# Lending finished mixer buffers to the rows of u and v in a two-layer diffusion backbone

## The chip, the core and the metric

The kernel runs on one core of one Trainium2 chip. The metric is the time of one execution on the device in microseconds (us). The core's engines are TensorE (PE; its weight loads are listed as PEld), VectorE (DVE), ScalarE (ACT), GpSimd (POOL) and SyncE (SP). Transfers go through 16 DMA engines; those of this text are issued by SP (weights) and by POOL (gathers of rows).

## What is computed

Two layers run over 256 latent tokens and 256 context tokens of width 1024, in float32. Each layer has a token mixer (window attention, differential attention, a convolution and a pooling branch, each with a gate) and then a feed-forward part that looks up experts. The change concerns the second part, `peer_ffn`:

```python
q = (xc @ wq).reshape(PEER_CHUNK, PEER_HEADS, 2, PEER_DKEY // 2)
...
gate = jax.nn.softmax(sc.astype(jnp.float32), axis=-1).astype(xc.dtype)
u = jnp.take(u_tab, idx, axis=0)
act = jax.nn.gelu(jnp.einsum('td,thkd->thk', xc, u), approximate=False)
v = jnp.take(v_tab, idx, axis=0)
return jnp.einsum('thk,thkd->td', gate * act, v)
```

Each token has 8 heads, each head picks 16 of 16384 experts. So each token needs 128 rows of u and 128 rows of v, 4 KB each.

## The kernel before, in words

The tokens are four tiles of 128: tiles 0 and 1 are context, 2 and 3 latents. Layer 1 runs the expert part for all four, layer 2 only for the latents, so there are six passes of it. A pass is the generator `gather` (L1114): for h = 0 to 8 it hands out 16 slots each. Slot k of step h fetches row h*16+k of u (`u_slot`, L1001, up to h = 7) and row (h-1)*16+k of v (`v_slot`, L1016, from h = 1): the v rows run one head behind, since their weights need the whole head. The first 16 slots are thus u alone and the last 16 v alone.

One gather (L998) is one instruction of POOL: it takes 128 indices and fetches one 4 KB row for each partition into a tile of 128 x 1024. A u row is multiplied by the token's vector and summed by one DVE instruction (L1006). After 16 of them `weigh` (L1009) forms the weights on ACT and DVE. A v row is either added to a sum by DVE (L1023) or multiplied with a diagonal matrix by PE (four matmuls of L1030, the matrix made by ACT, L1028). Which of both is fixed for each pass: in the latents' first pass of a layer (`few`) every fourth row goes to DVE, in the second (`half`) every second one. `add` (L1041) puts the sums into the tokens at the pass's end.

The rows lie in tiles of the tag "u" or "v" with GB = 5 places each. A gather may start when the row that was in its place has been read: by DVE for u, by DVE or PE for v.

The indices come from `route` (L1053), one head at a time: products with the query weights and the keys on PE, then `select` (L919), a search for the 16 best on DVE. In the latents' passes the routes of the following heads run beside the first pass (`side`), one at each step h. In layer 1 their weights come through the tag "w". In layer 2 those of heads 0 to 5 are fetched earlier and kept (`keep_q`, L1381) in tiles that the mixer no longer needs: head 0 in kc0 and vc0, head 1 in kc1 and vc1, head 2 in a tile hT, head 3 in two tiles q, head 4 in ys2 and ys3, head 5 in hk and ys0. ys1 is read by the mixer's last product, `mix(1, 1)`.

A pass that stands in the list `behind` is handed out in small portions while other work is emitted: `pump(us)` adds us times `credit[1]`, and each SLOT_US = 2.9 hands out a slot. `drain()` hands out the rest at once. The layer-1 latents start with a drain of the context's pass (L1313), then come both their passes (L1315, L1316). In layer 2 the first pass is put into `behind` at L1410 with RATE2 = 0.753; then `mix(1, 1)` (8 products, 1.8 each), `out_proj` (8 products, 2 each) and one `norm_T` (4) are emitted, the routes of heads 2, 0 and 1 (the last two for tile 3 alone), and the drain (L1419); the second pass is L1420.

The framework puts the instructions of each engine into an order when the program is built. It goes by the order of emission and by when it reckons data and places to be there, so an instruction that waits can be passed by later ones. On the chip each engine then keeps to that order.

Of the kernel before, what the change touches and what calls it, by code (L numbers as in the profile page):

```python
# [8 lines left out]
F = mybir.dt.float32  # L9
# [8 lines left out]
D = 1024  # L18
# [19 lines left out]
GB = 5  # L38
# [10 lines left out]
def body(ctx: ExitStack, tc: tile.TileContext, x_d, cc_d, cols_d, rows_d, w_mod, w_in, w_gate,  # L49
# [5 lines left out]
    sb = ctx.enter_context(tc.tile_pool(name="sb", bufs=1))  # L55
    pp = ctx.enter_context(tc.tile_pool(name="ps", bufs=1, space=bass.MemoryType.PSUM))

    def mm_ps():
        return pp.tile([128, 512], F, tag="mm", name="mm", bufs=2)
# [4 lines left out]
    def tr_ps():  # L64
        return pp.tile([128, 512], F, tag="tr", name="tr", bufs=2)
# [4 lines left out]
    def t2():  # L70
        return sb.tile([128, 512], F, tag="t2", name="t2", bufs=4)

    def m4(w=T):
        return sb.tile([128, 4, w], F, tag="m4", name="m4", bufs=3)
# [79 lines left out]
    def drain():  # L154
        while behind:
            for _ in behind.pop(0):
                pass
# [66 lines left out]
    def wtile(src, kb=KB, c=256, like=None):  # L224

        src = src.rearrange("(k p) c -> p k c", p=128)
        w = wplace(kb, c)
        nc.sync.dma_start(w, src)
        if not isinstance(like, Split):
            return w  # L230
        return Split(parts_of(w), row_places(kb // 2), row_places(kb // 2))
# [85 lines left out]
    def hslot():  # L317
        return sb.tile([128, KB, T], F, tag="hT", name="hT", bufs=3)
# [403 lines left out]
    def ch_proj(hT, l, c0, w=None):  # L722

        N = hT.shape[2]
        w = w or wtile(w_in[l, :, c0:c0 + 256], like=hT)
        ps = mm_ps()
        for b in range(2):
            product(ps[:, b * N:(b + 1) * N], w, slice(b * 128, (b + 1) * 128), hT, slice(0, N))
        tick(TICKS[0])
        pump(N * 7 / T)  # L730
        return ps[:, :2 * N].rearrange("p (b t) -> p b t", b=2)
# [68 lines left out]
    def pool_in(hT, l, ws=(None,) * 2):  # L800
        PAD = 16
        W = T + 2 * PAD
        u = m4(W)
        nc.vector.memset(u[:, :, :PAD], 0.0)  # L804
        nc.vector.memset(u[:, :, PAD + T:], 0.0)
        for i in range(2):
            pd = ch_proj(hT, l, O_DI + i * 256, ws[i])
            nc.scalar.copy(u[:, 2 * i:2 * i + 2, PAD:PAD + T], pd)
        return u

    def pool(u, l, out_):

        PAD = 16
        W = T + 2 * PAD
        pw = t2().rearrange("p (g c) -> p g c", g=4)
        nc.sync.dma_start(pw, pool_w[l].rearrange("g c e -> c g e"))

        a = m4(W)
        src = u
        for g, win in enumerate(WINS):  # L820
            w = W - win + 1
            h = win // 2
            nc.vector.tensor_tensor(a[:, g:, :w], src[:, g:, :w], src[:, g:, h:h + w], op=OP.add)
            lo = PAD - h
            y = t2()[:, :T]
            nc.vector.tensor_tensor(y[:, :8], a[:, g, lo:lo + 8], rcp[:, g, :8], op=OP.mult)
            nc.scalar.mul(y[:, 8:T - 8], a[:, g, lo + 8:lo + T - 8], 1.0 / win)
            nc.vector.tensor_tensor(y[:, T - 8:], a[:, g, lo + T - 8:lo + T], rcp[:, g, 8:], op=OP.mult)
            nc.vector.tensor_tensor(y, y, u[:, g, PAD:PAD + T], op=OP.subtract)
            ps = tr_ps()  # L830
            nc.tensor.matmul(ps[:, :T], pw[:, g, :], y, start=True, stop=True)
            nc.scalar.activation(out_[:, g, :], ps[:, :T], AF.Copy, scale=cols[:, l, C_PS + g:C_PS + g + 1])
            src = a
            yield
# [129 lines left out]
    def second_layer():  # L964

        nc.vector.tensor_scalar(places16[:, 0], places16[:, 0], float(NEXP // 128), None, op0=OP.add)

    class Tile:


# [23 lines left out]
            self.dacc = sb.tile([128, D], F, tag="dacc", name="dacc", bufs=1)  # L994

        def row(self, table, tag, j):
            r = sb.tile([128, D], F, tag=tag, name=tag, bufs=GB)
            nc.gpsimd.indirect_dma_start(out=r, out_offset=None, in_=table,  # L998
                                         in_offset=bass.IndirectOffsetOnAxis(ap=self.idx[:, j:j + 1], axis=0))
            return r  # L1000
# [52 lines left out]
    def route(ts, l, h, hT, c0, later=None, w=None):  # L1053

        w = w or wtile(w_q[l, :, h * 256:(h + 1) * 256])
        kt = sb.tile([128, 256], F, tag="kt", name="kt", bufs=1)
        nc.sync.dma_start(kt, kt_d[l, :, h])
        N = len(ts) * 128
        qT = []
        for b in range(2):  # L1060
            ps = mm_ps()
            product(ps[:, :N], w, slice(b * 128, (b + 1) * 128), hT, slice(c0, c0 + N))
            q = sb.tile([128, T], F, tag="qT", name="qT", bufs=2)
            nc.scalar.copy(q[:, :N], ps[:, :N])
            qT.append(q)
        jobs, scs = [], []
        for i, t in enumerate(ts):
            sp = mm_ps()
            for b in range(2):
                nc.tensor.matmul(sp[:, b * 128:(b + 1) * 128], qT[b][:, i * 128:(i + 1) * 128],  # L1070
                                 kt[:, b * 128:(b + 1) * 128], start=True, stop=True)
            sc = sb.tile([128, 256], F, tag="sc", name="sc", bufs=2)
            nc.scalar.copy(sc, sp[:, :256])
            if later is not None and t.t == 1:
                nc.scalar.dma_start(later[h], sc)
                continue
            jobs.append((t, h))
            scs.append(sc)
        if jobs:
            select(jobs, scs)  # L1080
# [20 lines left out]
    def waited(t, later):  # L1101

        for h in range(0, 8, 2):
            scs = [sb.tile([128, 256], F, tag="sc", name="sc", bufs=2) for i in range(2)]
            for i, sc in enumerate(scs):
                nc.scalar.dma_start(sc, later[h + i])
            select([(t, h), (t, h + 1)], scs)
            yield 1
            yield 1

    def gather(t, on_dve, nxt=None, side=()):

        side = iter(side)
        t.begin(on_dve)  # L1114
        for h in range(9):
            next(side, None)
            if h == 8:
                t.gates()
            for k in range(16):
                if h < 8:  # L1120
                    t.u_slot(h * 16 + k)
                if h > 0:
                    t.v_slot(h * 16 - 16 + k)
                yield 1
            if h < 8:
                t.weigh(h)
            if h == 7 and nxt:
                nxt.prepare()
        for _ in side:
            pass  # L1130
        t.add(t.va.rearrange("p a b -> p (a b)"))

    def ysb(n):
        return sb.tile([128, 4, T], F, tag=f"ys{n}", name=f"ys{n}", bufs=1)
# [43 lines left out]
    def part(y, n):  # L1178
        return y[:, :, n * 128:(n + 1) * 128]
# [16 lines left out]
    def pieces(gen, n):  # L1196

        pending.extend([lambda: next(gen, None)] * n)
# [3 lines left out]
    ys = [ysb(n) for n in range(4)]  # L1202
    alloc_kv((1,))
    u = pool_in(hc, 0)
# [12 lines left out]
    def every(*gens):  # L1217
        for g in gens:
            for _ in g:
                pass  # L1220
# [36 lines left out]
    def place(tag, bufs=1):  # L1257
        return sb.tile([128, D], F, tag=tag, name="wk", bufs=bufs).rearrange("p (k c) -> p k c", k=4)

    places = [[place("dacc"), place("h2", 2)]] + [[place("v", GB) for i in range(2)] for j in range(2)]  # L1260
# [4 lines left out]
    h = hslot()  # L1265
# [12 lines left out]
    u = pool_in(h, 0, ws[4:6])  # L1278
    alloc_kv((0,))
    ys = [ysb(n) for n in range(4)]  # L1280
# [29 lines left out]
    tsl = []  # L1310
    rl = router((2, 3), 0, tsl)
    next(rl)
    drain()  # L1313

    every(gather(tsl[0], P_L0, tsl[1], rl))  # L1315
    every(gather(tsl[1], P_L1, tsc[1], waited(tsc[1], later)))  # L1316


    behind.append(gather(tsc[1], P_C1))
    credit[1] = RATE1  # L1320
    h = norm_T((2, 3), 1, 0)
    hx = norm_T((0,), 1, 0, hk())
    alloc_kv((0, 1))
    yb = conv_in(h, 1)
    u = pool_in(h, 1)
    pieces(pool(u, 1, ys[3]), 5)
    pieces(conv(yb, 1, ys[2]), 16)
    kv_proj(h, 1, hx)
# [27 lines left out]
    def cut(n):  # L1356
        return slice(n * 128, (n + 1) * 128)

    def mix(n, br):
        th = (tha, thc)[br]  # L1360
        branches(part(ys[br], n), 128, lambda blk: th[blk // 4][:, blk % 4, cut(n)], accT[:, :, cut(n)], wbr[br])
# [37 lines left out]
    route(tsl[:1], 1, 0, hT, 0, w=wq[0])  # L1399
    tsl[0].prepare(True)  # L1400

    def routes():

        yield 1
        yield 1
        for h in range(3, 8):
            route(tsl, 1, h, hT, 0, w=wq[h] if h < len(wq) else None)
            yield 1

    behind.append(gather(tsl[0], P_F0, tsl[1], routes()))  # L1410
    credit[1] = RATE2
    mix(1, 1)
    route(tsl[:1], 1, 1, hT, 0, w=wq[1])
    out_proj(accT[:, :, cut(1)], (3,), 1, wout)
    norm_T((3,), 1, 1, hT, 128)
    route(tsl, 1, 2, hT, 0, w=wq[2])
    for h in range(2):
        route(tsl[1:], 1, h, hT, 128, w=wq[h])
    drain()  # L1419
    every(gather(tsl[1], P_F1))  # L1420

# [2 lines left out]
    for n in range(2):  # L1424
        r = st8()[:, 7:8]
# [68 lines left out]
```

## Time and profile before

| what | value |
|---|---|
| median of 3 runs | 3164.84 us (3161.33 to 3167.96) |
| the profiled execution | 3163.87 us |
| its span, first to last instruction | 3162.1 us |
| DVE busy | 2332.2 us (74%) |
| PE busy | 2358.6 us (75%) |
| POOL busy | 1760.0 us (56%) |
| gathers of u, busy on POOL | 768, 869.1 us, mean 1132 ns |
| gathers of v, busy on POOL | 768, 890.3 us, mean 1159 ns |
| DMA bytes | 1036.55 MB, of which gathers 805.40 MB |

Shares of the span are averages over stages with different limits. The latents' passes are at 1016 to 1784 us (layer 1) and 2391 to 3145 us (layer 2). The trace lists for each idle time of an engine what ended it; "issue" is time in which it waited for nothing that the trace shows. Between two gathers POOL always has such a step of about 0.3 us.

### The profile page before, as it was taken

How to read it: one execution, taken by the hardware profiler on the slowest of the kernel's cores; microseconds unless marked ns; L12 is line 12 of the kernel's file. 1: busy time of each engine (PE TensorE's matmuls, PEld its weight loads, DVE VectorE, ACT ScalarE, POOL GpSimd, SP SyncE). 2: the span in 40 equal slices, each digit the busy share in tenths (PEclk: the TensorE clock that was granted, in tenths of full speed). 3: DMA queues.
4: the chain of work that ended last, by engine and by line, in shares of the span. 5: the costliest groups of instructions: out<-in, count | busy, mean ns of one | idle time of the engine just before them, and what ended most of it. 6: DMA issues, size and time to landing. Idle time of an engine off the chain costs nothing.

```text
span 3162.1 us, 33260 instructions
## 1 busy us (share of the span) xinstructions
PE 2358.6 (75%) x10524; PEld 1568.2 (50%) x10524; DVE 2332.2 (74%) x5221; ACT 667.9 (21%) x1577; POOL 1760.0 (56%) x1542
## 2 busy tenths in 40 slices
PE   7999998889867776675555479679997876545555
PEld 5878887667755552222111267557686542211111
DVE  5956569778977899856677659876657995556776
ACT  3455421224112121110000111023332221110001
POOL 0000037544555577777777657666405687767775
PEclk9999999999988897786788799889998987977868
DMA  9948969887899899998999999999957899989998
GB/s 307 318 142 263 315 229 322 300 306 263 316 359 335 310 391 326 334 375 323 396 409 407 332 336 384 322 346 354 344 167 264 290 325 366 397 315 397 407 408 312
DMA packets 436782, 1036.55 MB, mean 328 GB/s; under 512 B 30464, under 2 KB 226560, under 8 KB 436608
## 3 DMA queue, kind: packets, MB, share of 16 engines
q0 software_dynamic: 221184, 805.40, 67.9%
q1 hardware_dynamic: 211984, 226.25, 21.5%
q10 hardware_dynamic: 3440, 2.78, 0.3%
q8 instruction: 84, 1.38, 0.2%
q14 instruction: 90, 0.74, 0.1%
HBM read 1032.22 MB, written 2.10 MB: 327 GB/s over the span
## 4 chain that ended last, share of the span: by engine, by line
PE 29%; issue 23%; DVE 22%; DMA 18%; POOL 7%; ACT 1%; ACTq 0%; POOLq 0%; DVEq 0%
PE mm L215 12%; DVE u L1006 6%; DMA v<-in_v_dram,idx 6%; DMA u<-in_u_dram,idx 4%; DMA w<-in_w_gate_dram 4%; POOL u L998 3%; POOL v L998 3%; PE va L1030 3%; DVE m L774 3%; DVE dacc L1023 3%; DMA w<-in_w_in_dram 2%; PE mm L213 2%; PE mm L211 2%; PE mm L212 2%; PE at L473 2%
## 5 line engine op out<-in xcount | busy, mean ns | idle before, releaser
L998 POOL DMA_INDIRECT u<-in_u_dram,idx x768 | 869.1, 1132 | 919.0 <-DVE m L804 430.9
L1030 PE MATMUL va<-v,dg 128*128 128x512 f32 x1436 | 871.0, 745 | 568.7 <-DMA v<-in_v_dram,idx 493.0
L1006 DVE SCALAR_TENSOR_TENSOR u<-u,h 128x1024 f32<-128x1024 f32 x768 | 934.7, 1220 | 328.3 <-DMA u<-in_u_dram,idx 326.2
L998 POOL DMA_INDIRECT v<-in_v_dram,idx x768 | 890.3, 1159 | 465.0 <-issue 172.7
L1030 PEld LDWEIGHTS va<-v,dg 128*128 128x128 f32 x1436 | 304.7, 230 | 1071.4 <-issue 853.4
L1023 DVE SCALAR_TENSOR_TENSOR dacc<-v,wt,dacc 128x1024 f32<-128x1024 f32 x403 | 515.9, 1280 | 105.5 <-DMA v<-in_v_dram,idx 91.0
L215 PE MATMUL mm<-hT,w 128*128 128x256 f32 (+1 forms) x2176 | 512.4, 387 | 108.1 <-DMA w<-in_w_gate_dram 70.5
L215 PEld LDWEIGHTS mm<-hT,w 128*128 128x128 f32 x2176 | 407.9, 204 | 184.7 <-issue 69.6
L1028 ACT ACTIVATE dg<-ident,wt 128x128 f32<-128x128 f32 x359 | 141.5, 400 | 965.8 <-PE va L1030 906.0
L774 DVE SCALAR_TENSOR_TENSOR m<-m,cols,m 128x256 f32<-128x256 f32 x360 | 158.0, 475 | 0.1
L212 PE MATMUL mm<-hT,whi 128*128 128x256 f32 x512 | 143.9, 281 | 0.8 <-DVE hT L174 0.8
L211 PE MATMUL mm<-hT,whi 128*128 128x256 f32 x448 | 128.1, 286 | 4.0 <-ACT whi L173 3.2
L213 PE MATMUL mm<-hT,whi 128*128 128x256 f32 x448 | 127.2, 284 | 1.2 <-DVE whi L174 0.8
L215 PE MATMUL mm<-w,hT 128*128 128x256 f32 x512 | 116.3, 386 | 9.4 <-DMA w<-in_w_in_dram 9.4
L174 DVE TENSOR_TENSOR whi<-w,whi 128x1024 fp32r<-128x1024 f32 x86 | 104.1, 1222 | 17.6 <-ACT whi L173 10.3
L215 PEld LDWEIGHTS mm<-w,hT 128*128 128x128 f32 x512 | 98.5, 194 | 25.0 <-issue 11.2
L173 ACT CAST whi<-w 128x1024 fp32r<-128x1024 f32 x86 | 88.4, 1048 | 68.0 <-PE mm L213 46.3
L215 PE MATMUL mm<-ys,w 128*128 128x256 f32 x384 | 95.0, 385 | 4.6 <-ACT th L844 4.0
L212 PEld LDWEIGHTS mm<-hT,whi 128*128 128x128 f32 x512 | 97.4, 190 | 1.7 <-DVE hT L174 1.0
L844 ACT ACTIVATE th<-mm,cols 128x256 f32<-128x256 f32 x80 | 37.9, 474 | 261.6 <-PE mm L215 204.8
L211 PEld LDWEIGHTS mm<-hT,whi 128*128 128x128 f32 x448 | 85.6, 191 | 6.4 <-ACT whi L173 4.0
L213 PEld LDWEIGHTS mm<-hT,whi 128*128 128x128 f32 x448 | 85.1, 190 | 6.8 <-DVE whi L174 3.6
(339 smaller groups left out, 2821.3 us busy)
## 6 DMA issues: line engine op xcount, KB each, us to landing
w<-in_w_gate_dram SPq DMA_DIRECT2D x48, 1024.0 KB, 10.7
w<-in_w_in_dram SPq DMA_DIRECT2D x42, 1024.0 KB, 10.6
X<-in_w_mod_dram SPq DMA_DIRECT2D x40, 512.0 KB, 5.2
wm<-in_w_mod_dram SPq DMA_DIRECT2D x40, 512.0 KB, 5.3
w<-in_w_branch_dram SPq DMA_DIRECT2D x20, 1024.0 KB, 8.0
w<-in_w_q_dram SPq DMA_DIRECT2D x20, 1024.0 KB, 12.0
u<-in_u_dram,idx POOLq DMA_INDIRECT x768, 6.5
v<-in_v_dram,idx POOLq DMA_INDIRECT x768, 6.5
```

What stands on the lines that cost most here:

```text
L173: nc.scalar.copy(hi.bitcast(FR), v)
L174: nc.vector.tensor_tensor(lo.bitcast(FR), v, hi, op=OP.subtract)
L211: nc.tensor.matmul(ps, ah, bh, start=first, stop=False)
L212: nc.tensor.matmul(ps, ah, bl, start=False, stop=False)
L213: nc.tensor.matmul(ps, al, bh, start=False, stop=last)
L215: nc.tensor.matmul(ps, a[:, kb, ca], b[:, kb, cb], start=first, stop=last)
L774: nc.vector.scalar_tensor_tensor(acc[:, b, :], yb[:, b, k:k + T], cols[:, l, cw + k:cw + k + 1], acc[:, b, :], op0=OP.mult, op1=OP.add)
L998: nc.gpsimd.indirect_dma_start(out=r, out_offset=None, in_=table, in_offset=bass.IndirectOffsetOnAxis(ap=self.idx[:, j:j + 1], axis=0))
L1006: nc.vector.scalar_tensor_tensor(r, r, 1.0, self.h2, op0=OP.mult, op1=OP.mult, accum_out=self.act[:, j % 16:j % 16 + 1])
L1023: nc.vector.scalar_tensor_tensor(self.dacc, v, w, self.dacc, op0=OP.mult, op1=OP.add)
L1028: nc.scalar.activation(dg, ident, AF.Copy, scale=w)
L1030: nc.tensor.matmul(self.va[:, half, :], dg, v[:, half * 512:(half + 1) * 512], start=j == self.pe[0], stop=j == self.pe[-1])
```

## The change

A list of tags for each table, `places_of`, says where the next rows go, in turn. `row` takes its tile from `row_place`. For layer 1's latents u gets seven more places (ys0 to ys3, two of q, hk) and v four (kc0, vc0, kc1, vc1), lent before the drain; `give_back` returns to five and five after the second pass. Layer 2 then allocates its ys tiles anew, where before it wrote into those of layer 1. In layer 2 places are lent one after the other: ys1 after `mix(1, 1)`, and those of kept query weights each time the last route that reads them has been emitted. At the end u has 14 and v 7.

```diff
+    places_of = {"u": ["u"] * GB, "v": ["v"] * GB}
+    turn = {"u": 0, "v": 0}
+
+    def lend(**more):
+
+        for tag, places in more.items():
+            places_of[tag].extend(places)
+
+    def give_back():
+        for tag in "uv":
+            places_of[tag] = [tag] * GB
+            turn[tag] = 0
+
+    def row_place(tag):
+        at = places_of[tag]
+        place = at[turn[tag] % len(at)]
+        turn[tag] += 1
+        return sb.tile([128, D], F, tag=place, name=tag, bufs=GB if place in "uv" else 2 if place == "q" else 1)
...
         def row(self, table, tag, j):
-            r = sb.tile([128, D], F, tag=tag, name=tag, bufs=GB)
+            r = row_place(tag)
...
     next(rl)
+    lend(u=["ys0", "ys1", "ys2", "ys3", "q", "q", "hk"], v=["kc0", "vc0", "kc1", "vc1"])
     drain()
 
     every(gather(tsl[0], P_L0, tsl[1], rl))
     every(gather(tsl[1], P_L1, tsc[1], waited(tsc[1], later)))
+    give_back()
...
     u = pool_in(h, 1)
+    ys = [ysb(n) for n in range(4)]
     pieces(pool(u, 1, ys[3]), 5)
...
+    freed = {0: dict(u=["kc0"], v=["vc0"]), 1: dict(u=["kc1", "vc1"]), 3: dict(u=["q", "q"]),
+             4: dict(u=["ys2"], v=["ys3"]), 5: dict(u=["hk", "ys0"])}
+
     def routes():
 
         yield 1
         yield 1
         for h in range(3, 8):
             route(tsl, 1, h, hT, 0, w=wq[h] if h < len(wq) else None)
+            lend(**freed.get(h, {}))
             yield 1
 
     behind.append(gather(tsl[0], P_F0, tsl[1], routes()))
     credit[1] = RATE2
     mix(1, 1)
+    lend(u=["ys1"])
     route(tsl[:1], 1, 1, hT, 0, w=wq[1])
...
     for h in range(2):
         route(tsl[1:], 1, h, hT, 128, w=wq[h])
+        lend(**freed[h])
     drain()
     every(gather(tsl[1], P_F1))
```

## Rows read from the trace of the kernel before

**Rows 1.** Stretches: PE, PEld, DVE, ACT, POOL busy us, TensorE clock, DMA share, GB/s.
```profile
1100.00:1240.00 140.00, 104.23 (x316) 57.45 (x316) 138.52 (x464) 26.57 (x63) 100.86 (x86) 0.88 0.99 369
1240.00:1300.00 60.00, 36.93 (x56) 12.72 (x54) 59.79 (x212) 8.14 (x18) 49.03 (x37) 0.74 0.91 317
1300.00:1404.00 104.00, 71.00 (x112) 25.77 (x112) 61.74 (x98) 13.37 (x33) 81.45 (x74) 0.79 0.98 365
1404.00:1447.00 43.00, 31.85 (x77) 14.13 (x76) 18.99 (x27) 7.42 (x19) 23.61 (x26) 0.89 0.90 328
...
1500.00:1750.00 250.00, 132.63 (x193) 43.97 (x192) 177.46 (x247) 20.56 (x54) 191.21 (x193) 0.81 1.02 404
...
2465.00:2600.00 135.00, 111.37 (x377) 66.58 (x376) 130.60 (x445) 28.03 (x68) 104.62 (x82) 0.93 0.90 319
```

**Rows 2.** Waits of POOL, 1016 to 1105 us: total us, times, longest.
```profile
POOL u L998 <- DVE u L1006: 10.2, 8, 3.5
...
POOL v L998 <- PE va L1030: 6.2, 2, 5.4
```

**Rows 3.** Waits of POOL, 1105 to 1240 us.
```profile
POOL v L998 <- PE va L1030: 8.2, 8, 2.2
POOL u L998 <- DVE u L1006: 6.2, 7, 1.7
```

**Rows 4.** Waits of POOL, 1240 to 1404 us.
```profile
POOL v L998 <- PE va L1030: 1.8, 6, 0.3
...
POOL u L998 <- DVE u L1006: 0.6, 1, 0.6
```

**Rows 5.** POOL's timeline: tile ends' u rows, and the last v row.
```profile
1404.53 1.01 POOL L998 DMA_INDIRECT u<-in_u_dram,idx  x1 [0.31 <-issue]
...
1436.44 0.94 POOL L998 DMA_INDIRECT u<-in_u_dram,idx  x1 [0.30 <-issue]
...
1755.14 0.94 POOL L998 DMA_INDIRECT u<-in_u_dram,idx  x1 [0.30 <-issue]
...
1783.27 0.94 POOL L998 DMA_INDIRECT u<-in_u_dram,idx  x1 [0.31 <-issue]
...
2764.32 1.02 POOL L998 DMA_INDIRECT u<-in_u_dram,idx  x1 [0.30 <-issue]
...
2796.96 0.94 POOL L998 DMA_INDIRECT u<-in_u_dram,idx  x1 [0.30 <-issue]
...
3115.32 0.94 POOL L998 DMA_INDIRECT u<-in_u_dram,idx  x1 [0.30 <-issue]
...
3143.65 0.94 POOL L998 DMA_INDIRECT v<-in_v_dram,idx  x1 [0.64 <-DVE dacc L1023]
```

**Rows 6.** Waits of POOL, 2510 to 2764 us, longest in total.
```profile
POOL v L998 <- PE va L1030: 3.0, 10, 0.3
```

**Rows 7.** Timeline of DVE and POOL near 1331 us, of PE at 1358.
```profile
1331.40 1.23 DVE L1006 SCALAR_TENSOR_TENSOR u<-u,h 128x1024 f32<-128x1024 f32 x1 [1.98 <-DMA u<-in_u_dram,idx]
1331.88 1.56 POOL L998 DMA_INDIRECT v<-in_v_dram,idx  x1 [0.30 <-issue]
...
1358.03 1.96 PE L1030 MATMUL va<-v,dg 128*128 128x512 f32 x4 [0.21 <-DMA v<-in_v_dram,idx]
```

**Rows 8.** DMA issues: count and median us from issue to landing.
```profile
v<-in_v_dram,idx POOLq DMA_INDIRECT x768, 6.5
```

**Rows 9.** Waits of POOL, 1404 to 1447 us.
```profile
POOL u L998 <- DVE u L1006: 3.3, 2, 2.6
```

**Rows 10.** Timeline of POOL and PE at the beginning of layer 2's latents.
```profile
2405.49 0.94 POOL L998 DMA_INDIRECT u<-in_u_dram,idx  x1 [1.73 <-DVE u L1006]
2434.78 2.07 PE L1030 MATMUL va<-v,dg 128*128 128x512 f32 x2 [17.27 <-ACT dg L1028]
2457.58 4.03 PE L215 MATMUL mm<-hT,wk 128*128 128x128 f32 x32
2462.97 1.83 POOL L998 DMA_INDIRECT v<-in_v_dram,idx  x1 [10.05 <-PE mm L1070]
```

## The prediction

> **What bounds the kernel now.** I read the stretches first. In the expert stages GpSimd (POOL) issues 256 gathers of 128 rows per tile (128 of u, 128 of v). Where nothing holds it, 193 gathers take 250 us, 1.295 us each, at 404 GB/s and a DMA share of 1.02 [rows 1]: the fastest pace the kernel knows. I call it the free pace; there the gathers themselves are the limit and no number of places helps.
>
> The two latent tiles of layer 1 hold POOL from about 1016 to 1784 us: 768 us for 512 gathers that would take 663 at the free pace. So some 105 us are not pace; in layer 2 it is 2391 to 3145, 754 us, so some 91. Then I asked where POOL loses them and what it waits for, since only a wait for a *place* can shrink.
> - 1016 to 1240 us: POOL waits for VectorE (DVE) to finish a u row (10.2 and 6.2 us) and for TensorE to finish a v row (6.2 and 8.2) [rows 2, 3]: 31 us, all waits for one of the five places per table. DVE is itself busy 138.5 of 140 us [rows 1].
> - 1240 to 1404 us: place waits are gone (0.6 us for u) [rows 4], yet a gather takes 1.62 us up to 1300 (60 us, 37) and 1.41 after (104 us, 74) [rows 1].
> - At the end of each tile: the last u row is issued, 17 v rows follow alone, then 16 u rows of the next tile alone. Five places per table hold POOL then. From the last u row to the next pass's first are 18 gathers: 31.9 us in layer 1, 32.6 in layer 2, and 28.1 at the end of layer 1's second tile; to the kernel's last v row are 17, 28.3 us [rows 5]. At the free pace 18 gathers take 23.3 us and 17 take 22.0.
> - Layer 2's first tile, 2510 to 2764: POOL waited for nothing longer than 0.3 us (the longest row sums ten such steps) [rows 6]. Only its first 70 us and its end can change.
>
> **The sum.** The added code issues no instruction on the chip: Python picks another tag, and DVE, TensorE, ScalarE and the transfers have the same work. What moves is the moment at which POOL may issue. The sum is against the profiled execution, 3163.87 us (span 3162.1); the median of the runs is 1 us above, so I add 1.
> 1. *First tile of layer 1.* u has 12 places, v 9. DVE sets the pace until 1300, so that end stays; what changes is how far POOL stands ahead then. u and v are issued in turn, so the shorter list counts: 9 pairs ahead for 5, 8 gathers. After 1300 POOL is behind DVE (61.7 of 104 us busy), so each gather already issued is worth its 1.41 us: 8 x 1.41 = 11. There is idle time to issue them in: 31 us of place waits [rows 2, 3]. Ends: 0, if the lead is used up before 1300, and 20, if all seven added u places count (14 gathers). I take 6, as gathers are dearer while DVE has a backlog (below).
> 2. *Layer 1, tile to tile.* The v rows become bound by TensorE: 12 of 16 go there (every fourth to DVE) at 1.96 us [rows 7], 24 us, rather than by five places and a landing of 6.5 us [rows 8]. 31.9 - 24 = 8. POOL's wait behind the first u rows (3.3 us, [rows 9]) goes as well, since 12 places hold them while DVE adds the tile up: 2.5. Together 10.5; ends 4 and 13.
> 3. *Layer 1, end of the second tile.* 28.1 - 23.3 = 5: half the rows go to each engine, 8 x 1.96 = 16 us, so TensorE doesn't bind. Ends 1 and 5. What follows is the mixer of layer 2, which needs the tile's sum: the stage is shifted whole.
> 4. *Background tile, layer 2's mixer:* 5 and 5 places again, nothing. The new ys tiles wait for u rows read long before: nothing; the cover is the 16 v rows behind them.
> 5. *Layer 2, beginning.* Here is the doubtful step. Counting the credit: 8 branch products x 1.8, 8 output products x 2 and one norm x 4 are 34.4, times 0.753 over 2.9 gives 8 slots handed out before the drain. Row 8 of u therefore gets place 8 of nine: vc1, which holds query weights of head 1 until tile 3's product of that head. That product starts at 2457.58 and takes 4.03 us, to 2461.6; the present kernel issued u rows at 2405.49 and fed the first v row to TensorE at 2434.78 [rows 10]. Head 0's v rows need all 16 u rows, so they come some 35 us later. The build lets other rows pass (rows 9 to 14 have free places), and POOL now stands still for 10 of those us anyway [rows 10]. I take 0 between -10 and +8.
> 6. *Layer 2, tile to tile.* 32.6 - 24 = 8.6, and 2.4 at the first u rows, as in 2: 11. Seven v places still carry it: 6.5 us landing and 2 of use over 7 rows are 1.2 us a row. Ends 4 and 14.
> 7. *End of the kernel.* 28.3 - 22 = 6; ends 2 and 6.
>
> Sum: 6 + 10.5 + 5 + 0 + 11 + 6 = 38.5, say 39 us: 3163.9 - 39 + 1 = **3126 us**. Who is late next: POOL, at its free pace, and at the tile ends TensorE.
>
> **Why gathers are dearer beside a busy DVE.** A gather usually takes 0.94 us. The one of 1331.88 took 1.56: a product of a u row had begun on DVE at 1331.40 and ended at 1332.63, and the gather ends 0.81 us after it [rows 7]. So a gather that starts inside a product waits it out. The Trainium skill's page "SBUF — State Buffer" (section "SBUF: two separate sides") says that DVE, in an instruction with two SBUF inputs, and GpSimd take one port pair as an exclusive lock, whoever starts first. The trace agrees, by that pair of instructions. By that rule a change that lets rows pile up in front of DVE makes DVE's products run back to back and so slows POOL; that is the second rival below.
>
> **Rivals.**
> - *The lent places stall POOL in layer 2 (slower).* Each engine runs in the order written at build time; if that order puts row 8 or a row in q, ys or hk before its weights are really read, POOL stands still with everything behind it. Price: held from 2405.5 to 2462.5, 57 us, of which it waits 10 today, so 47; and some 19 u products of 1.23 us [rows 7], 23 us, then fall into 2465 to 2600, where DVE is busy 130.6 of 135 us [rows 1]. 70 - 39 = 31 slower: 3196. It decides once the stall costs more than the 39 us of the other steps. For it: the 10 us wait on a route product [rows 10] shows that the built order can be wrong. Against: only one row in three of the first lists is lent before 2462. 0.14, of which 0.10 slower by over 0.2%.
> - *The port takes it back.* Rows land earlier, DVE runs dense, a gather costs 1.62 us as in 1240 to 1300 [rows 1]. 18 gathers then take 29.2, 17 take 27.5: the four tile ends give 2.7 + 0 + 3.4 + 0.8 = 7 us, step 1 nothing: 3158. For it: just that stretch. Against: in the tile ends DVE has few rows to do (19.0 of 43 us busy) [rows 1]. 0.14.
> - *More than forecast.* Steps 1, 2, 3, 5, 6, 7 at their upper ends: 20 + 13 + 5 + 8 + 14 + 6 = 66: 3099; by halves between that and the forecast, 3110. 0.12.
> - *It does nothing it says*: that rows never reach the lent places is excluded by the code, which cycles through the list from the drain on.
>
> **The numbers.** Forecast 0.60. About 0.2% (6 us) is what a measurement of this kernel tells from no change. Faster: 0.60 + 0.12 + 0.07 of the port case = 0.79; same: 0.07 of the port case and 0.04 of the stall = 0.11; slower 0.10. The range goes from 3099, the larger gain, to 3160, past the port case; the stall and what lies beyond all upper ends are left out, some 0.15.
>
> **What would show it.** Right: from the last u row of one latent tile to the first of the next some 24 us, in both layers; no place waits of POOL between 1016 and 1240; the first tile's last u row some 6 to 11 us before 1404. Step 5 is seen in layer 2's first v product on TensorE: after 2434 less the shift (about 22 us) by 35 us, with POOL busy on other rows. Wrong: a POOL wait of over 10 us for a route's product in layer 2, or gathers of over 1.5 us at the tile ends.

## The result, and the profile after

The changed kernel takes 3127.54 us (median of 4 runs, 3111.36 to 3133.77) against 3166.4 us before beside it: a ratio of 0.9855, interval 0.982 to 0.9889, or 39 us. The forecast was 39 us, 3126. The profiled execution took 3130.84 us, its span 3129.0, 33 us below the span before; that is the sum split up here.

The profile follows the chain of work that ended last back through the span. On it POOL's own share has gone from 7 to 16%, so the issuing of gathers weighs more than before; PE (28%) and DVE (20%) still have larger shares.

Stretches of the changed kernel (columns as in [rows 1]):

```profile
1016.00:1100.00 84.00, 60.88 (x254) 44.00 (x252) 73.34 (x221) 17.63 (x41) 57.88 (x47) 0.89 0.89 323
1100.00:1240.00 140.00, 107.31 (x324) 59.14 (x324) 139.18 (x476) 27.45 (x65) 112.28 (x92) 0.87 1.01 386
1240.00:1300.00 60.00, 29.62 (x49) 11.66 (x49) 59.73 (x213) 8.42 (x20) 46.98 (x41) 0.75 0.98 362
1300.00:1391.00 91.00, 64.36 (x104) 24.57 (x104) 59.54 (x93) 12.15 (x30) 70.95 (x61) 0.79 0.95 347
...
1500.00:1735.00 235.00, 130.84 (x183) 40.62 (x181) 166.78 (x231) 19.33 (x51) 179.66 (x182) 0.78 1.02 404
...
2600.00:2739.00 139.00, 81.31 (x164) 28.34 (x162) 81.81 (x123) 18.23 (x45) 106.40 (x108) 0.98 1.02 403
```

The same of the kernel before, where [rows 1] has none:

```profile
1016.00:1100.00 84.00, 58.93 (x248) 43.56 (x247) 71.25 (x223) 17.23 (x40) 48.64 (x44) 0.89 0.85 298
...
2600.00:2764.00 164.00, 105.07 (x180) 37.83 (x178) 95.54 (x148) 20.51 (x50) 127.72 (x120) 0.86 0.99 377
```

Read the number of gathers behind POOL's busy time. Up to 1300 us it is 47 + 92 + 41 = 180 after and 44 + 86 + 37 = 167 before (the 44 from the row just above, the others from [rows 1]): POOL stands 13 gathers further, while DVE is as full as it was (139.18 and 59.73 us against 138.52 and 59.79). The free pace is the same, 235 us for 182, 1.29 us each.

Waits of POOL in the changed kernel, 1016 to 1105 us, the longest (answering to [rows 2]):

```profile
POOL u L1018 <- DVE h L1000: 14.8, 1, 14.8
POOL u L1018 <- DVE idx L958: 11.9, 1, 11.9
```

The first precedes the pass, the second is a wait for the indices of head 1: neither is a wait for a place. Of the place waits of [rows 2, 3], 31 us with POOL's usual step of 0.3 us ahead of each and 24 without it, none is left; from 1105 to 1240 us the longest sum besides "issue" is six steps of 0.3 us:

```profile
POOL v L1018 <- DMA v<-in_v_dram,idx: 1.8, 6, 0.3
```

POOL's timeline, the rows that answer to [rows 5]: last u row of a pass and first of the next, and the last v row:

```profile
1390.76 1.09 POOL L1018 DMA_INDIRECT u<-in_u_dram,idx  x1 [0.30 <-issue]
...
1415.84 0.94 POOL L1018 DMA_INDIRECT u<-in_u_dram,idx  x1 [0.30 <-issue]
...
1735.09 0.94 POOL L1018 DMA_INDIRECT u<-in_u_dram,idx  x1 [0.30 <-issue]
...
1758.11 1.00 POOL L1018 DMA_INDIRECT u<-in_u_dram,idx  x1 [0.30 <-issue]
...
2739.49 1.00 POOL L1018 DMA_INDIRECT u<-in_u_dram,idx  x1 [0.30 <-issue]
...
2766.17 1.32 POOL L1018 DMA_INDIRECT u<-in_u_dram,idx  x1 [0.30 <-issue]
...
3086.84 0.94 POOL L1018 DMA_INDIRECT u<-in_u_dram,idx  x1 [0.30 <-issue]
...
3110.17 1.61 POOL L1018 DMA_INDIRECT v<-in_v_dram,idx  x1 [0.30 <-issue]
```

At the first of these ends POOL waited for TensorE before the change, 1404 to 1447 us, and no longer does after it, 1391 to 1417 us; what is left are steps of 0.3 us:

```profile
POOL v L998 <- PE va L1030: 10.5, 9, 2.0
```

```profile
POOL v L1018 <- PE va L1050: 0.6, 2, 0.3
```

With the first u rows of the passes (1016.20 and 2391.30 before, 1016.52 and 2373.63 after; 1783.27 and 1758.11 begin the background pass) these marks cut the span into pieces. All figures are us; "first" and "second" run from the first to the last u row of a pass, "between" from there to the next pass's first u row, "mixer" from the first u row of the background pass to that of layer 2's first latent pass, "end" from the last u row to the last v row:

| | layer 1: first | between | second | to background | mixer | layer 2: first | between | second | end |
|---|---|---|---|---|---|---|---|---|---|
| before | 388.3 | 31.9 | 318.7 | 28.1 | 608.0 | 373.0 | 32.6 | 318.4 | 28.3 |
| changed | 374.2 | 25.1 | 319.3 | 23.0 | 615.5 | 365.9 | 26.7 | 320.7 | 23.3 |
| gain | 14.1 | 6.8 | -0.5 | 5.1 | -7.5 | 7.1 | 5.9 | -2.3 | 5.0 |

That is 33.8 by the unrounded marks; what lies ahead of 1016 and behind the last v row took 0.8 more, which leaves the span's 33.

The gain of the first pass has two parts. Between its first and last u row, 239 gathers, POOL was idle for 108.1 us before and for 86.4 after, 21.7 less: the place waits are gone. The gathers themselves took 280.2 us before and 287.9 after, 7.7 more. That leaves the 14.

At the beginning of layer 2 the forecast wait of rows in lent places can be seen. POOL and TensorE of the changed kernel (answering to [rows 10]):

```profile
2430.62 0.94 POOL L1018 DMA_INDIRECT u<-in_u_dram,idx  x1 [8.47 <-PE mm L215]
...
2453.06 10.57 PE L1050 MATMUL va<-v,dg 128*128 128x512 f32 x24
```

A gather into a lent place waits 8.47 us for a route's product, by its time that of tile 3's head 0, and the second gather after it 2.29 us for that of head 1, whose weights lie in the place of row 8. The first v row reaches TensorE 79.4 us after the pass's first u row instead of 43.5, 36 us later in its pass (forecast 35). Yet the pass is not longer.

### The profile page after: what moved, and what is told of

It is laid out like the page before. It is cut to its first block, busy times and chain, and to the rows that moved or that the text cites. A ratio compares the mean times of both kernels' runs of the same rounds, so it can differ in the third digit from the quotient of the medians.

```text
span 3129.0 us, 32834 instructions
## 1 busy us (share of the span) xinstructions
PE 2336.2 (75%) x10524; PEld 1561.6 (50%) x10524; DVE 2330.6 (74%) x5221; ACT 667.8 (21%) x1577; POOL 1744.7 (56%) x1542
## 3 DMA queue, kind: packets, MB, share of 16 engines
q1 hardware_dynamic: 211984, 226.25, 21.7%
## 4 chain that ended last, share of the span: by engine, by line
PE 28%; DVE 20%; issue 18%; DMA 17%; POOL 16%; ACT 1%; SPq 0%; ACTq 0%; POOLq 0%; DVEq 0%
PE mm L215 12%; POOL v L1018 10%; POOL u L1018 6%; DMA v<-in_v_dram,idx 5%; DVE u L1026 5%; DMA w<-in_w_gate_dram 4%; DMA u<-in_u_dram,idx 3%; DVE m L774 3%; DVE dacc L1043 2%; PE mm L213 2%; PE mm L211 2%; DMA w<-in_w_in_dram 2%; PE mm L212 2%; PE at L473 2%; PE va L1050 2%
## 5 line engine op out<-in xcount | busy, mean ns | idle before, releaser
L1018 POOL DMA_INDIRECT u<-in_u_dram,idx x768 | 859.9, 1120 | 933.9 <-DVE m L804 428.9
L1050 PE MATMUL va<-v,dg 128*128 128x512 f32 x1436 | 843.4, 725 | 533.1 <-DMA v<-in_v_dram,idx 450.6
L1050 PEld LDWEIGHTS va<-v,dg 128*128 128x128 f32 x1436 | 295.9, 222 | 1023.6 <-issue 789.8
```

The costliest lines, as they stand in the source:

```text
L1050: nc.tensor.matmul(self.va[:, half, :], dg, v[:, half * 512:(half + 1) * 512], start=j == self.pe[0], stop=j == self.pe[-1])
```

## The experiments

The theory: POOL loses time where a row's place is not free, and each added place is worth something only there. The rivals: another instruction order as a whole; rows in lent places that stall layer 2; the port between DVE and POOL that takes back what the places give. The three groups of runs (1 to 4, 5 to 8, 9 to 12) ran on chips 4, 0 and 2, on which the kernel before took 3244, 3244 and 3239 us, 2.4% more than in the comparison above (whose chip the record doesn't name). There the free pace is about 1.42 us a gather (260 us, 180 to 186 gathers) at 364 to 374 GB/s, and the gain of the whole change is smaller. So ratios are read within a group, and marks against runs of these chips that left that layer as it was. Marks come from one execution of each run, ratios from several; no profile of the kernel before was taken on these chips.

**1. Layer 1 alone.** `freed` is emptied and ys1 not lent.

```diff
-    freed = {0: dict(u=["kc0"], v=["vc0"]), 1: dict(u=["kc1", "vc1"]), 3: dict(u=["q", "q"]),
-             4: dict(u=["ys2"], v=["ys3"]), 5: dict(u=["hk", "ys0"])}
+    freed = {h: {} for h in range(8)}
...
-    lend(u=["ys1"])
```

Expected:

> Places are lent in layer 1 alone; layer 2 keeps five and five. Theory (POOL waits for places, each place where it is lent): the layer-1 latents shrink as in the changed kernel, first pass from 388 to about 374 us between its first and last u row, 32 to 25 us to the second pass, 28 to 23 us at its end, 25 us in all; layer 2's passes are those of before (373, 33, 318, 28 us). About 25 us faster than before, ratio 0.992. Rival (the gain comes from another instruction order as a whole, not from places at their spot): layer 1 gains by another amount, or layer 2's passes move too.

Measured: ratio 0.9939 (0.991 to 0.9968). In layer 1 the tile ends take 29.9 and 26.0 us (30.8 and 32.9 in run 2, which has five and five there). The first pass takes 388.2 us, more than expected. 224 us into it POOL had issued 137 gathers, as in the changed kernel (135 to 139) and against 128 in runs 2 and 3. Then one wait of 11.0 us for TensorE, which itself stood 14.7 us until ACT had made its matrix, took about half of that lead back. Layer 2 is as before but for that chip's pace: 379.0, then 30.5, end 31.4. So layer 1's places gain by themselves, and layer 2 doesn't move.

**2. Layer 2 alone.**

```diff
-    lend(u=["ys0", "ys1", "ys2", "ys3", "q", "q", "hk"], v=["kc0", "vc0", "kc1", "vc1"])
```

Expected:

> Places are lent in layer 2 alone. Theory: layer 1 as before (388, 32, 319, 28 us); in layer 2 first pass 366 us, 27 us to the second, 23 us at the end, as in the changed kernel: 16 us faster than before, ratio 0.995. Head 0's first v row reaches TensorE some 55 to 60 us after the pass's first u row (before: 43), since row 8 of u waits for the route of tile 3's head 1. Rival (that wait costs more than the tile ends give): no gain or a loss.

Measured: ratio 0.9961 (0.9941 to 0.998). Between the passes 28.0 and at the end 23.4 us instead of 30.5 to 33.7 and 29.1 to 31.4 in the four runs with five and five there. The first pass takes 384.8, no gain; the first v row comes 83.9 us after the pass began, later than expected. The kernel gains nonetheless, so the rival is out. The product of both ratios is 0.990.

**3. Layer 1, lent only for the tile ends.** The side generator lends when step 8 of the first pass begins.

```diff
+    def at_end(side):
+        for h in range(9):
+            if h == 8:
+                lend(u=["ys0", "ys1", "ys2", "ys3", "q", "q", "hk"], v=["kc0", "vc0", "kc1", "vc1"])
+            next(side, None)
+            yield 1
+
-    every(gather(tsl[0], P_L0, tsl[1], rl))
+    every(gather(tsl[0], P_L0, tsl[1], at_end(rl)))
```

Layer 2 as in 1, and the lending ahead of the drain is left out. Expected:

> Layer 1 alone, and its places are lent only when the last 16 v rows of the first pass are handed out. Theory: the first pass is that of before (388 us from first to last u row), the two tile ends shrink to about 25 and 23 us; 11 to 12 us faster than before, ratio 0.996. So the first pass's 14 us would be the lead that POOL gains while DVE sets the pace. Rival (the first pass's gain comes from its first rows or its last ones alone): the first pass gains here too, some 5 us or more.

Measured: first pass 395.9 us, the tile ends 25.8 and 26.3, against 30.8 and 32.9 in run 2; ratio 0.9989 (0.9968 to 1.0009). So the tile ends shrink as expected, but the kernel as a whole shows no gain clear of noise, and the 0.996 expected lies outside the interval. The second pass, 353.5 us against 346.6 in run 2, took more than half of it back; why, no run shows. The first pass has no gain here, nor in run 2 (392.5); with places from the start it takes 376.1 to 388.2 (runs 1, 4, 5, 9), and 224 us into it POOL is 7 to 11 gathers further (135 to 139 against 128). Its gain is therefore earned while it runs, and apart from that of its end.

**4. Layer 2 without early rows in places that are still read.**

```diff
-    freed = {0: dict(u=["kc0"], v=["vc0"]), 1: dict(u=["kc1", "vc1"]), 3: dict(u=["q", "q"]),
+    freed = {0: {}, 1: {}, 3: dict(u=["q", "q", "kc0", "kc1", "vc1"], v=["vc0"]),
```

Expected:

> As the changed kernel, but in layer 2 kc0, kc1, vc0 and vc1 are lent only with q, from the third head on; no early row waits for kept weights. Theory (the wait of rows in lent places is made good later, as other rows pass them and DVE sets the pace until the routes end): the first v row reaches TensorE about 43 us after the pass's first u row instead of 79 us, and the first pass takes 364 to 370 us from first to last u row, as in the changed kernel (366). Rival (that wait costs time): the pass falls to 358 us or less, and the kernel is 8 us or more faster than the changed one.

Measured: the first v row reaches TensorE 47.2 us after the pass's first u row, and the first pass takes 380.7 us; in the changed kernel (runs 5, 9) these are 82.6 and 83.4 us, and 384.3 and 380.5. Ratio 0.9934 (0.9904 to 0.9963), within that of the changed kernel. So 35 us of delay for the first v row cost 0 to 4 us. The 364 to 370 us expected were of the first chip's pace.

**5. The changed kernel again.**

> The changed kernel once more, beside the following ones. Theory (the gains of the layers add): ratio to the kernel before about that of layer 1 alone times that of layer 2 alone, 0.994 x 0.996 = 0.990. Head 0's first v row of layer 2 reaches TensorE about 80 us after the pass's first u row, and the latents' first passes take about 374 to 381 and 366 to 385 us from first to last u row.

Measured: 0.993 (0.99 to 0.996); with run 9, 0.990 (0.9873 to 0.9926). The product of runs 1 and 2, 0.990, lies in both intervals (at the edge of the first), which agrees with gains that add. It is no proof: run 1's 0.9939 lies in the first as well.

**6. Only u gets places** (layer 1 alone).

```diff
-    lend(u=["ys0", "ys1", "ys2", "ys3", "q", "q", "hk"], v=["kc0", "vc0", "kc1", "vc1"])
+    lend(u=["ys0", "ys1", "ys2", "ys3", "q", "q", "hk"])
```

> Layer 1 alone, seven more places for u, none for v. The prediction's step 1 says that the shorter list counts, since u and v are issued in turn: then POOL gets no lead in the first pass (388 to 396 us from first to last u row, place waits for v as before) and the tile ends keep 28 to 32 us, since five v places hold the lone v rows: ratio 0.999 to 1.000. Rival (the lists count each for itself, as rows pass each other in POOL's order): the first pass gains 5 us or more, and u rows of the next pass are issued among the last v rows.

Measured: first pass 388.1, tile ends 31.9 and 32.2 us, ratio 0.9966 (0.9927 to 1.0004). The tile ends are those of before. POOL's groups of gathers, 1018 to 1390 us (count, busy, mean ns, idle before and what ended it):

```profile
L1018 POOL DMA_INDIRECT v<-in_v_dram,idx x102 | 112.5, 1103 | 56.7 <-issue 24.0 <-DVE dacc L1043 10.1 <-PE va L1050 10.0
```

v rows wait 20 us for places, as in the kernel before (17.7 us in the same stretch there); seven more for u leave that as it was, while the u rows' own place waits, 17.0 us there, are gone.

**7. Only v gets places** (layer 1 alone).

```diff
+    lend(v=["kc0", "vc0", "kc1", "vc1"])
```

> Layer 1 alone, four more places for v, none for u. By step 1 the first pass again gains nothing in its middle (five u places hold POOL); the tile ends gain, as their lone v rows have nine places: about 25 and 24 us, 10 us in all, ratio 0.997. Rival (u places are what the tile ends lack): they keep 30 and 28 us.

Measured: first pass 386.3, tile ends 26.7 and 25.0 us, ratio 0.9981 (0.9947 to 1.0015). The tile ends take all of their gain from v. By step 1 POOL should have gained no lead in the first pass; 224 us into it, it had issued 134 gathers, against 128 in runs 2 and 3, 131 in run 6 and 135 to 139 with both lists longer (runs 1, 4, 5, 9). The same group, the u row of it:

```profile
L1018 POOL DMA_INDIRECT u<-in_u_dram,idx x120 | 141.0, 1175 | 68.5 <-DVE u L1026 29.5 <-issue 20.2 <-DVE ix L909 4.4
```

Now u rows wait 29.5 us behind DVE. So neither list is simply the shorter one: four v places alone give 6 gathers of lead, seven u places alone 3, both together 7 to 11. Each of these is one execution, and the pass times of runs 6 and 7 (388.1 and 386.3) don't tell them apart, nor from run 1's 388.2.

**8. Products of half length.** In layer 1's latents the product of a u row takes 512 of the 1024 columns (the other half of each dot product is left out).

```diff
-            nc.vector.scalar_tensor_tensor(r, r, 1.0, self.h2, op0=OP.mult, op1=OP.mult,
+            c = 512 if self.l == 0 and self.t >= 2 else D
+            nc.vector.scalar_tensor_tensor(r[:, :c], r[:, :c], 1.0, self.h2[:, :c], op0=OP.mult, op1=OP.mult,
```

> As the changed kernel, but in the latents of layer 1 the product of a u row with the token's vector takes only the first 512 of 1024 columns, so the second half of each dot product is left out. The transfers are the same. Theory (a gather that starts while such a product runs waits until its end): with products of 0.6 instead of 1.2 us the time by which that layer's gathers exceed 0.94 us falls to half or less in the first pass (57 to 67 us before and after) and DVE no longer sets the pace, so the first pass takes 350 us or less from first to last u row. Rival (the gathers are stretched by full rings of the DMA engines, whatever DVE does): the excess stays above 50 us.

Measured, the same groups of gathers, 1018 to 1390 us; first the changed kernel of run 5, then this one:

```profile
L1018 POOL DMA_INDIRECT u<-in_u_dram,idx x123 | 151.7, 1233 | 52.8 <-issue 33.2 <-DVE idx L958 15.6 <-DMA v<-in_v_dram,idx 1.2
L1018 POOL DMA_INDIRECT v<-in_v_dram,idx x109 | 123.4, 1132 | 45.2 <-issue 25.6 <-DVE dacc L1043 8.4 <-PE va L1050 4.2
```

```profile
L1018 POOL DMA_INDIRECT u<-in_u_dram,idx x121 | 127.2, 1051 | 77.1 <-issue 34.8 <-DVE idx L958 23.9 <-DVE h L1000 16.3
L1018 POOL DMA_INDIRECT v<-in_v_dram,idx x104 | 105.5, 1014 | 79.3 <-issue 25.6 <-DVE dacc L1044 19.3 <-PE va L1051 12.5
```

Summed over 256 gathers from the first pass's first on, the time above 0.94 us falls from 61 to 24 us: a gather is stretched by DVE's products and not by full rings. But the pass takes 391.8 us and not 350. The time moved into waits for v places (19.3 and 12.5 us). DVE also stood 25.7 us in two waits, one of them 13.9, ahead of the weights without a cause in the trace. This is a single execution. So this run gives the stretch, not the price of it.

**9. The changed kernel once more**, for the next three.

> The changed kernel beside the three that follow. As in the runs before: ratio to the kernel before 0.986 to 0.993; first pass of layer 1 374 to 381 us, tile ends 25 to 30 and 23 to 26 us, first pass of layer 2 366 to 384 us.

Measured: 0.990 (0.9873 to 0.9926).

**10. v rows of heads 0 to 3 to TensorE** in the first passes.

```diff
+    rest = lambda j: j >= 64 and few(j)
-    P_C0, P_L0, P_L1, P_C1, P_F0, P_F1 = (lambda j: j < 48 or (j * 15) % 16 < 15), few, half, most, few, half
+    P_C0, P_L0, P_L1, P_C1, P_F0, P_F1 = (lambda j: j < 48 or (j * 15) % 16 < 15), rest, half, most, rest, half
```

> As the changed kernel, but in the latents' first passes the v rows of heads 0 to 3 all go to TensorE; before, every fourth went to DVE: 16 DVE instructions of 1.28 us less and 16 rows of 1.96 us more on TensorE in each first pass. Theory (the routes' searches on DVE set the pace until about 1300 us; the places only decide how far POOL gets ahead): DVE's busy stretch ends some 15 to 20 us earlier and each first pass is 8 to 15 us shorter, 16 to 30 us in all, ratio to the changed kernel 0.991 to 0.995. Rival (v places, held until TensorE or DVE has read them, set the pace, and TensorE is slower with a row than DVE): no gain or a loss of a few us in each.

Measured: 0.994 (0.9903 to 0.9978), no faster than run 9, first passes 384.7 and 391.6 us against 376.1 and 380.5. The waits of POOL for TensorE, 1100 to 1240 us, and TensorE's row near the end of the longest of them:

```profile
POOL v L1018 <- PE va L1050: 17.3, 10, 10.7
```

```profile
1197.68 0.77 PE L1090 MATMUL mm<-kt,qT 128*128 128x128 f32 x2 [6.80 <-DMA kt<-in_kt_dram]
```

The theory failed: DVE has time to spare now (busy 123.2 of 140 us, 139.8 in run 9), and the pass is no shorter. POOL waits 17.3 us for TensorE to read v rows, as the rival has it. But 10.7 of them are one wait, and in it TensorE didn't work on rows: it stood 6.8 us until a route's keys had landed. So the trace shows that POOL waits for v places while DVE has time to spare; that TensorE's slower rows set the pace is not shown.

**11. The lists exchanged:** nine places for u and twelve for v in layer 1, nine and twelve at the end of layer 2.

```diff
-    lend(u=["ys0", "ys1", "ys2", "ys3", "q", "q", "hk"], v=["kc0", "vc0", "kc1", "vc1"])
+    lend(u=["kc0", "vc0", "kc1", "vc1"], v=["ys0", "ys1", "ys2", "ys3", "q", "q", "hk"])
...
-    freed = {0: dict(u=["kc0"], v=["vc0"]), 1: dict(u=["kc1", "vc1"]), 3: dict(u=["q", "q"]),
-             4: dict(u=["ys2"], v=["ys3"]), 5: dict(u=["hk", "ys0"])}
+    freed = {0: dict(u=["kc0"], v=["vc0"]), 1: dict(v=["kc1", "vc1"]), 3: dict(v=["q", "q"]),
+             4: dict(u=["ys2"], v=["ys3"]), 5: dict(u=["hk"], v=["ys0"])}
```

> As the changed kernel with the lists exchanged: in layer 1 four of the lent places go to u and seven to v (9 and 12 instead of 12 and 9); in layer 2 at the end u has 9 and v 12 instead of 14 and 7. Theory (v is the shorter list: its rows wait for the weights of their whole head): POOL's place waits for v behind DVE's sums go, its lead grows by up to 3 pairs, the tile ends of layer 2 reach those of layer 1: 3 to 10 us faster than the changed kernel. Rival (the free pace and DVE already set everything, no place is short any more): within 3 us of it.

Measured: 0.9913 (0.988 to 0.9946), run 9's 0.990 within it; first passes 375.1 and 381.4 us against 376.1 and 380.5. So exchanging the lists changes nothing beyond noise, which is the rival. Its reason holds only in part. With nine u places POOL waits again for DVE to read u rows, 6.5 us in layer 1's first pass and 4.9 in its second, where the changed kernel of run 9 has no such wait. In layer 2 the stretch between the passes is shorter (24.4 us against 27.6) and the end longer (32.4 against 23.8); 4.0 us of that end is one wait for something that is none of the core's engines.

**12. Runs 10 and 11 together.**

> Both edits together: the v rows of heads 0 to 3 to TensorE, and the lent places exchanged. Theory: the gains add, 20 to 35 us faster than the changed kernel. Rival: no more than the better of the two.

Measured: 0.9947 (0.9923 to 0.9972), no better than run 10; first passes 386.3 and 384.6 us. The gains don't add. In the first pass no v row waits for a place any more, but u rows, with nine places, wait 16.0 us: the wait has changed lists. No version here that computes the same beats the changed kernel.

## Why the prediction was right, step by step

The mechanism was the forecast one: DVE, TensorE and the transfers do the same work, and POOL's waits for places are what went. The sum was met more closely than its terms, and that was in part luck: in the profiled pair the two first passes gave 21.2 us for 6 forecast, the tile ends with the second passes 20.0 for 32.5, and the mixer lost 7.5 for nothing forecast.

1. *First tile of layer 1: 6 forecast, 14.1 measured.* The lead was 13 gathers, not 8: 13 x 1.41 would be 18. A gather after 1300 took 1.49 us (91 us, 61) instead of 1.41, some 5 us over the 61; the rest stayed. The step that failed is "the shorter list counts". Runs 6 and 7 speak against it, with one trace each: u alone gives 3 gathers, v alone 6, both 7 to 11. The discount from 11 to 6 was too large.
2. *Layer 1, tile to tile: 8 forecast for the v rows, 6.8 measured.* 25.1 us is near the 24 forecast, but not for the reason given: in this stretch no gather waits more than 0.31 us, so TensorE doesn't bind, and TensorE itself waits for rows (1.78, 0.79 and 1.59 us). The forecast let TensorE's twelve of the 16 rows set the time, though nine places let POOL run ahead of it. 18 gathers of 0.94 us and 0.30 between them are 22.4 us; three that took 1.50 to 1.99 make up most of the rest. On the chips of the experiments POOL still waits 1.4 to 3.0 us for TensorE there beyond its steps (runs 1, 4, 5, 9). The 2.5 us at the first u rows didn't come (-0.5): in the second pass POOL's idle time fell by 2.7 us, as forecast, and its gathers took 3.3 us more.
3. *End of the second tile: 5 forecast, 5.1 measured.*
4. *Mixer: nothing forecast, 7.5 lost.* The runs don't lay this on the places: the changed kernel itself took 602.4 and 621.2 us here in runs 5 and 9, all twelve lie between 600.6 and 621.2. All twelve have the new ys tiles of layer 2, so these were not tested by themselves. In this pair the first 500 us of the stage are alike and the last part differs, before and after:

```profile
2283.00:2391.00 108.00, 101.79 (x785) 93.62 (x784) 69.19 (x263) 38.01 (x149) 0.00 (x0) 1.00 0.51 167
```

```profile
2258.00:2374.00 116.00, 109.66 (x793) 100.37 (x794) 70.44 (x266) 38.59 (x151) 0.37 (x1) 0.94 0.47 160
```

TensorE has nearly the same work (793 and 785 matmuls) and is busy 7.9 us longer, at a mean granted clock of 0.94 instead of 1.00. Why it was lower, no run here shows.

5. *Beginning of layer 2: 0 forecast, 7.1 measured* in the profiled pair, and a loss of 3.6 us in the experiments (380.5 to 384.8, mean 383.2, in runs 2, 5, 9 against 378.1 to 381.4, mean 379.6, in runs 1, 3, 6, 7). Both lie in the range of -10 to +8. The stall came as worked out, 36 us for the first v row, and cost 0 to 4 us, as run 4 shows; other rows passed. Behind the small sum stand two larger terms that the prediction didn't have. In the pass POOL was idle 7.2 us more than before, and its gathers took 14.4 us less (261.7 us against 276.1). The chips of the experiments show the same two: idle 112 to 126 us with places lent in layer 2 (runs 2, 4, 5, 8, 9, 10, 12) and 100 to 104 without (1, 3, 6, 7), gathers 261 to 268 us and 275 to 280; run 11, with 104 and 278, is an exception. Why the gathers are shorter there, no run shows. So the 7.1 us were not forecast, and they came in the stretch of which the prediction said that it couldn't change: a gather took 1.29 us (139 us, 108) from 2600 on instead of 1.37 (164, 120).
6. *Layer 2, tile to tile: 8.6 and 2.4 forecast, 5.9 and -2.3 measured.* As in 2, the first u rows gave nothing. Seven v places carry the end a little less well than nine (26.7 us against 25.1): POOL waits 1.7 us for TensorE there beyond its steps, and once 2.2 us without a cause in the trace.
7. *End: 6 forecast, 5.0 measured.*

The rival of the stall (slower by 31 us) had the place and the delay right and the price wrong: it took POOL to stand still with all that is behind it, and POOL stood 8.5 and 2.3 us. The rival of the port was half right: in layer 1's first pass, where 21.7 us of idle time went, longer gathers took 7.7 back, not all. Nearly every gather that starts inside a u product waits it out: in the kernel before, 358 gathers begin with more than 0.13 us of such a product left, and 349 of them end 0.7 to 0.9 us after it; in that first pass the 33 gathers that begin while DVE runs nothing take 0.94 us each. The Trainium skill's page "SBUF — State Buffer" (section "SBUF: two separate sides") names the lock, which the one that starts first holds for its whole instruction. The traces agree where DVE starts first, and run 8 too, as the time above 0.94 us went from 61 to 24 us when the products were halved. Where the gather starts first they don't: in the kernel before, 614 u products begin while a gather runs and take 1.220 us, the 154 others 1.218.

## What to carry to other kernels

Look for what a queue's waits are *for* before adding buffers: a place is worth its wait, once, and only in a stage in which the transfers don't already run at their free pace. Two streams that are issued in turn need places together: in these traces a list that was left short kept its waits, whatever the other had. A buffer that is lent before its last reader is done delays the row in it, but costs little where other rows can pass it.

## What was not expected of the hardware

- The same kernel took 3239 to 3244 us on the three chips of the experiments instead of 3166. There the free pace is about 1.42 us a gather at 364 to 374 GB/s, not 1.295 at 404; what makes it slower, no run shows. The gain of the change is 0.7 to 1.0% there instead of 1.45%. A floor that lies higher, 25.6 us for 18 gathers, would make the tile ends gain less; that this is the whole difference is not shown.
- Halving the DVE products beside the gathers moved a gather's mean from 1233 and 1132 ns (u and v) to 1051 and 1014, and the pass was none the shorter, 391.8 us: other waits took the time.
- Gathers and DVE's products hinder each other one way only here: a gather that starts inside a product is stretched, a product that starts inside a gather is not.
